# A hybrid HGRN2 and retention layer on one core: places of side transfers, order of the opening, and how the rows of x are scaled

## The chip, the cores and the metric

The kernel runs on one core of one Trainium2 chip. The metric is the device time of one execution in microseconds (us); a kernel's time is the median over runs on the same chip. Engines are named as the profile names them: PE (TensorE, its matrix multiplications), PEld (its weight loads, beside PE), DVE (VectorE), ACT (ScalarE), POOL (GpSimd), SP (SyncE, which here only issues transfers). A "product" below is a group of 12 matmuls of 128x512 on PE, the unit in which the program counts.

## The reference, cut to what matters

SEQ is 2048 and D_MODEL 1024; everything is float32.

```
mod = silu(c) @ w_ada + b_ada ;  shift, scale, gate = split(mod, 3)
h = rms_norm(x, norm_g) * (1 + scale) + shift
proj = h @ w_in            # columns: hq hf hi hz | rq rk rv rz | ga gb
oA = hgrn2_chunkwise(hq, hf, hi, lower_bound)        # 8 heads, state 128x128
qB, kB = rotary(rq), rotary(rk)                      # pairs turned by cos, sin of the position
oB = retention_chunkwise(qB, kB, rv)                 # 8 heads, state 64x128
uA = headRMSNorm(oA) * silu(hz) ; uB = headRMSNorm(oB) * silu(rz)
m = sigmoid(ga) * uA + sigmoid(gb) * uB
x = x + gate * (m @ w_out)
out = rms_norm(x, final_g)
```

Two parts of it are what this case is about. `rms_norm` scales each row (position) of x by its own factor, 1 over the root of the mean square; the projection needs h with the features on the partitions, that is x turned. And `rotary` needs a table of cosines and one of sines over the positions.

## The kernel before, in words

**Tiling.** The positions are worked in two halves of 1024 (`sb` 0 and 1), each of two blocks of 512 (`tb`). Per half, 36 "quads" go one after another; a quad is a group of 256 columns of `w_in`. Its kind is a letter: `a` (hgrn2 q and f), `v` (values), `b` (retention q and k), `A` and `B` (the merge gates and the silu gates). A quad is a 2x2 block product (features in two halves, columns in two), done as seven products by Winograd's scheme: A11, A12, A22 are the blocks of h, S1 to S4 their sums, and `b1` to `b7` are the weights or their sums. Every operand is split into a high and a low part, and each product is three matmuls (high by high, high by low, low by high) for four feature tiles. The products go in the order 2 (of this quad), 7, 1 (of the next), 5, 4, 3, 6. Products 2, 5 and 5+3 leave partial results that later products need: `stash` (L482) copies a PSUM bank to an SBUF tile `c2_`, `c5_` or `c53_` of the ring with the tag `cc` (NCC buffers), and `after` (L495, L502, L506) adds them up. The weights of three products ahead are brought and split (`W.pump`, L421, L295, L296).

**What orders the work.** PE runs in the order in which the program is written: its instructions are pinned. On ACT, DVE, POOL and SP a scheduler chooses the order from dependences and from priorities (the order of the program, shifted by `tc.high_priority(offset=...)`). Buffers are rings by tag: a tile that is asked for while all buffers are in use waits for the last reader of the oldest. `tmp()` gives a tile of the ring `tp` (NTP buffers of 128x512 float32). `cc` and `tp` and `mu` (4 buffers) hold tiles of the same size.

**Lanes and side work.** Between the products, `bg` runs the recurrences as lanes, and one "side" generator at a time, which goes on by one step (one `yield`) per product. The side work of the first half is `next_h(1)` (L1029 on), started in quad 14: it makes h for the second half. For each row tile it loads x (`xt`), squares and sums it on ACT (L1042), makes the diagonal matrix of the factors on POOL (`dgr`, L1047), and multiplies it by ones on PE, so that `rb` holds the factors along the free axis. Then it loads the turned x (`xT`), multiplies by `rb` on DVE (L1058), applies scale and shift on ACT, and stores hT to DRAM. Last it loads hT tiles again and makes S1 to S4 (L1078 on). Between a load and its first use stand two yields. `change_h(1)` loads the sums back in quad 35, the last of the first half.

**Rotation tables.** In a `b` quad, `take_b` (L641) turns a block of q or k: four DVE operations with the tables `ct` and `sn` (L647 to L650). `load_rot` (L630) brings both for one block with transfers issued by POOL (L634, L636): for block 0 at product 2 of the quad, for block 1 at product 2 of the next quad. The turned result of one block is stored by SP (`ro`, or `c` itself; L655).

**The opening.** `opening()` (L1105) works quad 0 without Winograd, and products 1 and 2 of quad 1. Its row tiles of x, `xrow0` to `xrow7`, come by SP. `stats(t)` squares and sums a row tile on ACT (L1116), makes the factor on POOL (`rstd_of`, L174 to L177), and scales the row tile on ACT (L1119). `turned(tb, kt)` turns four 128x128 pieces with PE transposes (L74) into a PSUM bank `xps`, and ACT makes h out of it with scale and shift (L1137). The scale and the shift come from `ada` (L355): DVE multiplies and sums tiles `wa` of `w_ada`, which SP brings, with `scb`, the row of silu(c) that `row_of_c` spreads over the partitions. `prepare` is `ada`, `turned` and the split of h (`split_a`). `plain_step` and `product_step` are the matmuls. After the loop: the two results `after(2, 1)` and `after(1, 1)`, `lower_bounds` (a softmax on ACT and DVE), four `deliver`s (quad 0's results go to ACT at L579 on), and the loading of constants and tables.

## Time and profile before

| | |
|---|---|
| time, median of 3 runs | 2068.94 us (2067.6 to 2070.96) |
| the profiled execution, its own time | 2069.38 us |
| span in it | 2067.6 us |
| granted TensorE clock, mean | 0.982 |
| PE busy | 1948.0 us (94%) |
| PEld busy | 1578.1 us (76%) |
| DVE busy | 1411.8 us (68%) |
| ACT busy | 993.2 us (48%) |
| POOL busy | 271.8 us (13%) |
| bytes moved | 259.95 MB, mean 126 GB/s |

How to read the rows of the trace that follow in the prediction. A row of the timeline has the start in us from the span's start, the duration in us, the engine, the line of the kernel, the operation, `out<-in` by the program's names without numbers, partitions x elements, and the count; brackets at its end hold the time for which the engine stood idle before it and the instruction or transfer that released it. A row of the waits has the waiting operation, what released it, the total in us, how often, and the longest. A row of the windows has a stretch of the span and in it the busy time of each engine (with the instructions), the granted clock as a share of full speed, the share of the DMA engines' time, and GB/s. A row of one line's instructions has the shortest, median and longest duration in ns and the time from the first to the last.

### The profile page before, as it was taken

How to read it: one execution, taken by the hardware profiler on the slowest of the kernel's cores; microseconds unless marked ns; L12 is line 12 of the kernel's file. 1: busy time of each engine (PE TensorE's matmuls, PEld its weight loads, DVE VectorE, ACT ScalarE, POOL GpSimd, SP SyncE). 2: the span in 40 equal slices, each digit the busy share in tenths (PEclk: the TensorE clock that was granted, in tenths of full speed). 3: DMA queues.
4: the chain of work that ended last, by engine and by line, in shares of the span. 5: the costliest groups of instructions: out<-in, count | busy, mean ns of one | idle time of the engine just before them, and what ended most of it. 6: DMA issues, size and time to landing. Idle time of an engine off the chain costs nothing.

```text
span 2067.6 us, 40051 instructions
## 1 busy us (share of the span) xinstructions
PE 1948.0 (94%) x15108; PEld 1578.1 (76%) x15108; DVE 1411.8 (68%) x2677; ACT 993.2 (48%) x2434; POOL 271.8 (13%) x514
## 2 busy tenths in 40 slices
PE   3889899999999889999999999999999999999998
PEld 2668688887787767878777788877788878887887
DVE  4876767676767658586895767677857675768332
ACT  5725454554555434545634545544455445445332
POOL 1001211122013110101001110211011101110000
PEclk9989999999999999999999999999999999999999
DMA  9144524344453565424645424354434433246442
GB/s 305 25 108 120 141 75 108 98 131 131 140 144 114 155 173 168 133 83 138 179 103 130 130 63 109 101 145 136 118 105 124 121 84 117 70 128 188 155 147 86
DMA packets 453120, 259.95 MB, mean 126 GB/s; under 512 B 171712, under 2 KB 406208, under 8 KB 452928
## 3 DMA queue, kind: packets, MB, share of 16 engines
q1 hardware_dynamic: 286752, 172.89, 29.8%
q10 hardware_dynamic: 153120, 76.04, 12.9%
q0 software_dynamic: 13056, 8.47, 1.6%
q8 instruction: 119, 1.95, 0.4%
q14 instruction: 73, 0.60, 0.1%
HBM read 188.03 MB, written 69.21 MB: 124 GB/s over the span
## 4 chain that ended last, share of the span: by engine, by line
PE 39%; DVE 5%; DMA 5%; ACT 2%; issue 1%; POOL 1%; SPq 0%; ACTq 0%; POOLq 0%; DVEq 0%
PE x L71 14%; PE ops L71 8%; PE v L71 7%; PE y L71 3%; PE poh L71 1%; DVE b L296 1%; PE lv L71 1%; DMA ud<-ur 1%; PE rt L71 1%; DMA wg<-in_w_gate_dram 1%; DVE w L421 1%; PE uT L74 1%; PE por L71 1%; ACT b L295 1%; DMA rd<-ro 1%
## 5 line engine op out<-in xcount | busy, mean ns | idle before, releaser
L296 DVE TENSOR_TENSOR b<-w,b 128x512 fp32r<-128x512 f32 (+1 forms) x553 | 346.1, 634 | 291.5 <-ACT b L295 286.2
L71 PE MATMUL v<-S,b 128*128 128x512 f32 x1704 | 429.2, 401 | 11.6 <-ACT c L482 11.3
L71 PE MATMUL x<-S,b 128*128 128x512 f32 x1704 | 433.1, 399 | 2.4 <-DVE c L502 1.3
L71 PE MATMUL x<-A,b 128*128 128x512 f32 x1704 | 425.3, 397 | 6.6 <-ACT c L482 5.8
L295 ACT ACTIVATE b<-w 128x512 fp32r<-128x512 f32 (+1 forms) x553 | 316.6, 583 | 238.1 <-PE x L71 172.8
L71 PEld LDWEIGHTS v<-S,b 128*128 128x128 f32 x1704 | 320.5, 191 | 82.3 <-ACT c L482 15.1
L71 PEld LDWEIGHTS x<-A,b 128*128 128x128 f32 x1704 | 317.9, 190 | 73.5 <-ACT c L482 6.8
L71 PEld LDWEIGHTS x<-S,b 128*128 128x128 f32 x1704 | 312.1, 189 | 64.6 <-DVE b L296 2.0
L71 PE MATMUL y<-A,b 128*128 128x512 f32 x840 | 211.3, 400 | 13.2 <-DVE vt L596 8.6
L421 DVE TENSOR_TENSOR w<-w,w 128x512 f32<-128x512 f32 x284 | 194.6, 685 | 6.1 <-DMA w<-in_w_d_dram 1.7
L71 PEld LDWEIGHTS y<-A,b 128*128 128x128 f32 x840 | 157.8, 192 | 47.0 <-issue 7.2
L71 PE MATMUL ops<-wo,m 128*128 128x512 f32 x768 | 174.8, 390 | 0.0
L71 PEld LDWEIGHTS ops<-wo,m 128*128 128x128 f32 x768 | 144.0, 188 | 30.4 <-DVE m L301 0.4
L174 POOL TENSOR_SCALAR ssh<-ssh 128x1 f32<-128x1 f32 x128 | 46.9, 366 | 756.5 <-ACT uh L837 753.4
L482 ACT ACTIVATE c<-v 128x512 f32<-128x512 f32 x142 | 84.4, 594 | 116.0 <-PE v L71 94.1
L840 ACT ACTIVATE uh<-poh,rrh 128x128 f32<-128x128 f32 x128 | 47.0, 367 | 120.9 <-POOL rrh L177 120.9
L71 PEld LDWEIGHTS lv<-q,k 128*32 128x32 f32 (+1 forms) x5888 | 69.3, 109 | 46.7 <-issue 34.4
L71 PE MATMUL lv<-q,k 128*32 128x16 f32 (+2 forms) x5888 | 80.5, 187 | 21.6 <-DVE ad L798 10.8
L786 DVE TENSOR_TENSOR q<-q,f 128x512 f32<-128x512 f32 x112 | 76.8, 685 | 13.8 <-PE lv L71 13.6
L177 POOL TENSOR_TENSOR rrh<-ssh,mhalf 128x1 f32<-128x1 f32 x128 | 83.0, 648 | 10.5
L502 DVE TENSOR_TENSOR c<-c,x 128x512 f32<-128x512 f32 x71 | 48.7, 685 | 50.8 <-PE x L71 50.4
L176 POOL TENSOR_TENSOR ssr<-ssr,epsx 128x2 f32<-128x2 f32 x64 | 20.9, 326 | 458.7 <-ACT ur L837 458.6
(191 smaller groups left out, 2443.0 us busy)
## 6 DMA issues: line engine op xcount, KB each, us to landing
w<-in_w_d_dram ACTq DMA_DIRECT2D x128, 256.0 KB
w<-in_w_c_dram ACTq DMA_DIRECT2D x66, 256.0 KB
mu<-ud SPq DMA_DIRECT2D x64, 256.0 KB
w<-in_w_a_dram ACTq DMA_DIRECT2D x60, 256.0 KB
wa<-in_w_ada_dram SPq DMA_DIRECT2D x16, 512.0 KB
w<-in_w_b_dram ACTq DMA_DIRECT2D x32, 256.0 KB
vd<-vt SPq DMA_DIRECT2D x128, 64.0 KB
vdr<-vt SPq DMA_DIRECT2D x128, 64.0 KB
```

The lines of the kernel that those rows point to most:

```text
L71: return tc.keep_in_program_order(nc.tensor.matmul(**kw))
L74: return tc.keep_in_program_order(nc.tensor.transpose(**kw))
L174: G.tensor_scalar(out=ss, in0=ss, scalar1=n * EPS, scalar2=None, op0=ALU.add)
L176: G.tensor_tensor(out=ss, in0=ss, in1=eps, op=ALU.add)
L177: G.tensor_tensor(out=dst, in0=ss, in1=mhalf.broadcast_to([P, w]), op=ALU.pow)
L295: S.activation(out=t[0], in_=src, func=AF.Copy)
L296: return V.tensor_tensor(out=t[1], in0=src, in1=t[0], op=ALU.subtract)
L421: V.tensor_tensor(out=out, in0=x, in1=y, op=ALU.add)
L482: S.activation(out=t, in_=ps, func=AF.Copy)
L502: V.tensor_tensor(out=t, in0=t, in1=xb[q], op=ALU.subtract)
L786: V.tensor_tensor(out=qv, in0=qv, in1=tv[:, :, :, 0:1].broadcast_to([P, NU, nb, m]), op=ALU.mult)
L840: S.activation(out=dsts[i], in_=pos[i], func=AF.Copy, scale=rr[:, i : i + 1])
```

## The change

Four things change; the arithmetic of the reference is untouched.

1. Buffers: the ring `cc` has 4 buffers in place of 5, the ring `tp` 6 in place of 5.
2. The opening. The small loads `ng` and `bad` are issued ahead of the rows of x, and rows 4 to 7 behind the first two `wa` loads and the first four `stats`. `row_of_c` and `prepare` are put under a high priority, the four `deliver`s under `PEV` (600). The scaling of the rows on ACT (eight of 128x1024) goes; instead POOL makes for each row tile the diagonal matrix of its factors (`diag`, eight of 128x128, in two of the `mu` buffers), and PE multiplies the piece of x by this diagonal (64 float32 matmuls of 128x128) where it transposed it with the identity (64). `scp1` sits in another PSUM bank, `h0_3` in `tp` and not in `cc`.
3. `next_h`: three yields in place of two between a load and its use for `xt`, `xT` and two of the hT loads, so that a row tile takes 7 steps in place of 6 and the whole 144 in place of 112. The squares (L1042), the multiplications by `rb` (L1058) and three of the sums (L1078 and later) are pinned to the order of the program on their engines. `rb` moves from the ring `mu` to `tp`.
4. `load_rot` of block 1 is issued at product 6 of the same `b` quad, one product ahead of where it was.

```
-NCC = 5
-NTP = 5
+NCC = 4
+NTP = 6
...
+    pin = tc.keep_in_program_order
...
+    ng = const("ng", [P, KT], a["ng_t"])
+    bad = const("bad", [P, 2 * KT], a["bada_t"])
     for t in range(4):
         load_rows(t)
...
-            ps = bank(f"scp{i}", "v")
+            ps = bank(f"scp{i}", ("v", "lv")[i])
...
+    FIRSTS = 2000
...   next_h
-            rb = upool.tile([P, 512], F32, name=f"rb{b}", tag="mu", bufs=4)
+            rb = tmp(f"rb{b}")
...
-                yield
-                yield
+                for _ in range(3):
+                    yield
                 for i in range(2):
-                    S.activation(out=xt[i], in_=xt[i], func=AF.Square, accum_out=ss[:, i : i + 1])
+                    pin(S.activation(out=xt[i], in_=xt[i], func=AF.Square, accum_out=ss[:, i : i + 1]))
...
-                yield
-                yield
-                V.tensor_tensor(out=x, in0=x, in1=rb, op=ALU.mult)
+                for _ in range(3):
+                    yield
+                pin(V.tensor_tensor(out=x, in0=x, in1=rb, op=ALU.mult))
...
-            V.tensor_tensor(out=h22, in0=h21, in1=h22, op=ALU.subtract)
+            pin(V.tensor_tensor(out=h22, in0=h21, in1=h22, op=ALU.subtract))
             keep("S1", h22)
             h11 = load(0, j)
             yield
             yield
-            V.tensor_tensor(out=h21, in0=h11, in1=h21, op=ALU.subtract)
+            yield
+            pin(V.tensor_tensor(out=h21, in0=h11, in1=h21, op=ALU.subtract))
...   the same for h12 and S4
...   opening
-        was = {0: ada_load(0)}
-        scb = row_of_c()
-        was[4] = ada_load(4)
-        for t in range(4, 8):
-            load_rows(t)
+        diag = [upool.tile([P, 512], F32, name=f"diag{i}", tag="mu", bufs=4) for i in range(2)]
+        with tc.high_priority(offset=FIRSTS):
+            scb = row_of_c()
...   stats
-            S.activation(out=xrows[t], in_=xrows[t], func=AF.Copy, scale=r[:, 0:1])
+            G.tensor_scalar(
+                out=diag[t // 4][:, t % 4 * P : (t % 4 + 1) * P], in0=ident, scalar1=r[:, 0:1], scalar2=None, op0=ALU.mult
+            )
...   turned
-                PE.transpose(
-                    out=ps[:, n * P : (n + 1) * P], in_=xrows[4 * tb + n][:, kt * P : (kt + 1) * P], identity=ident
+                t = 4 * tb + n
+                PE.matmul(
+                    out=ps[:, n * P : (n + 1) * P], lhsT=xrows[t][:, kt * P : (kt + 1) * P],
+                    rhs=diag[t // 4][:, t % 4 * P : (t % 4 + 1) * P], start=True, stop=True,
                 )
...
-                x = upool.tile([P, 512], F32, name="h0_3", tag="cc", bufs=NCC)
+                x = tmp("h0_3")
...   prepare: its three steps under tc.high_priority(offset=FIRSTS)
+        was = {0: ada_load(0), 4: ada_load(4)}
         for t in range(4):
             stats(t)
+        for t in range(4, 8):
+            load_rows(t)
...
-        for ch, tb in ((0, 0), (1, 0), (1, 1), (0, 1)):
-            deliver(0, ch, tb, acc[ch, tb])
+        with tc.high_priority(offset=PEV):
+            for ch, tb in ((0, 0), (1, 0), (1, 1), (0, 1)):
+                deliver(0, ch, tb, acc[ch, tb])
...   the loop over the products
-        if m == 2 and QUADS[q - 1][1] == "b":
-            load_rot(q - 1, 1)
+        if kind == "b" and m == 6:
+            load_rot(q, 1)
```

On ACT the opening's rows of the second block before: `sqj` is a square with its sum, `xrow` the scaling of a row tile, `h0_...` the making of h from a turned piece `xps`, `A12` and `A11` the split.

```order
L1137 ACTIVATE h0_0_302<-xps0_4_365,mods_120 128x512
L1119 ACTIVATE xrow4_89<-xrow4_89,x0r4_348 128x1024
L1116 ACTIVATE sqj_259,x0ss5_352<-xrow5_90 128x1024
L295 ACTIVATE A12_0_0_371<-h0_0_302 128x512
L1119 ACTIVATE xrow5_90<-xrow5_90,x0r5_354 128x1024
L1116 ACTIVATE sqj_259,x0ss6_383<-xrow6_91 128x1024
L1137 ACTIVATE h0_1_407<-xps0_1_402,mods_120 128x512
L1119 ACTIVATE xrow6_91<-xrow6_91,x0r6_385 128x1024
L1116 ACTIVATE sqj_259,x0ss7_389<-xrow7_92 128x1024
L295 ACTIVATE A11_0_1_409<-h0_1_407 128x512
L1119 ACTIVATE xrow7_92<-xrow7_92,x0r7_391 128x1024
L1137 ACTIVATE h0_1_0_417<-xps1_0_412,mods_120 128x512
```

The same place on ACT now, from behind the first square of the second block on:

```order
L1142 ACTIVATE h0_0_304<-xps0_0_299,mods_116 128x512
L1117 ACTIVATE sqj_245,x0ss5_354<-xrow5_280 128x1024
L295 ACTIVATE A11_0_0_306<-h0_0_304 128x512
L1117 ACTIVATE sqj_245,x0ss6_385<-xrow6_282 128x1024
L1142 ACTIVATE h0_0_304<-xps0_4_367,mods_116 128x512
L1117 ACTIVATE sqj_245,x0ss7_391<-xrow7_284 128x1024
L295 ACTIVATE A12_0_0_373<-h0_0_304 128x512
L1142 ACTIVATE h0_1_0_419<-xps1_0_414,mods_116 128x512
L295 ACTIVATE A21_0_0_421<-h0_1_0_419 128x512
L1142 ACTIVATE h0_1_409<-xps0_1_404,mods_116 128x512
L295 ACTIVATE A11_0_1_411<-h0_1_409 128x512
```

The four scalings of row tiles are out from between the squares, and the first h of the second block (`h0_1_0`, from `xps1_0`) stands two rows behind the last square, with `h0_1` behind it and not ahead.

On DVE in the first `b` quad (quad 2) before: `q0_0` and `k0_0` are steps of lane 0, `sw0_0_0` and `c2_2` the turning of block 0, `vt0_0_0_1` the turning of values on which a matmul of the lane waits.

```order
L786 TENSOR_TENSOR q0_0_764<-q0_0_764,f0_0_762 128x64x8
L421 TENSOR_TENSOR w3_0_998<-w3_0_998,w3_1_1088 128x512
L647 TENSOR_TENSOR sw0_0_0_1051<-c2_2_967,sn2_0_898 64x512
L421 TENSOR_TENSOR w3_1_1088<-w3_1_1088,w3_3_1090 128x512
L648 TENSOR_TENSOR sw0_0_0_1051<-c2_2_967,sn2_0_898 64x512
L787 TENSOR_TENSOR k0_0_763<-k0_0_763,f0_0_762 128x64x8
L649 TENSOR_TENSOR c2_2_967<-c2_2_967,ct2_0_897 128x512
L790 TENSOR_TENSOR k0_0_763<-k0_0_763,f0_0_762 128x64
L650 TENSOR_TENSOR c2_2_967<-c2_2_967,sw0_0_0_1051 128x512
L791 TENSOR_TENSOR f0_0_762<-f0_0_762 128x2x32
L596 STREAM_TRANSPOSE vt0_0_0_1_1144<-x1_345 128x512
```

The same place on DVE now:

```order
L296 TENSOR_TENSOR b2_3_1148<-w3_2_882,b2_3_1148 128x512
L787 TENSOR_TENSOR q0_0_766<-q0_0_766,f0_0_764 128x128x4
L648 TENSOR_TENSOR sw0_0_0_1053<-c2_2_969,sn2_0_900 64x512
L788 TENSOR_TENSOR k0_0_765<-k0_0_765,f0_0_764 128x128x4
L799 COPY_PREDICATED ad_110<-msk_72,lv0_0_4_1108 128x32x4
L791 TENSOR_TENSOR k0_0_765<-k0_0_765,f0_0_764 128x64
L792 TENSOR_TENSOR f0_0_764<-f0_0_764 128x2x64
L296 TENSOR_TENSOR b7_2_1170<-w2_1_832,b7_2_1170 128x4x64 x2
L597 STREAM_TRANSPOSE vt0_0_0_1_1146<-x1_347 128x512
L503 TENSOR_TENSOR c53_2_1163<-c53_2_1163,x2_996 128x512
L296 TENSOR_TENSOR b1_3_1242<-w3_0_1000,b1_3_1242 128x512
```

The values' turning `vt0_0_0_1` no longer stands behind the whole turning of block 0 (its three other rows come later now), while the first of those four rows, which needs the table `sn2_0`, now stands ahead of the lane's `k0_0` at L788.

On DVE at the turn from quad 23 to quad 24, a `b` quad, before: `xT3_2` and `xT3_3` are side steps, `c2_24` the stash of product 2, `sw0_3_0` the turning of block 0 of quad 24 with the tables `sn24_0` and `ct24_0`, `b3_24` to `b2_25` split weights.

```order
L596 STREAM_TRANSPOSE vt1_6_0_1_7401<-c5_23_7222 128x512
L1058 TENSOR_TENSOR xT3_2_7374<-xT3_2_7374,rb3_6060 128x512
L495 TENSOR_TENSOR c2_24_7376<-x24_7403,c2_24_7376 128x512
L296 TENSOR_TENSOR b3_24_7434<-w24_3_7232,b3_24_7434 128x4x64 x2
L296 TENSOR_TENSOR b6_24_7463<-w24_0_7126,b6_24_7463 128x4x64 x2
L647 TENSOR_TENSOR sw0_3_0_7428<-c2_24_7376,sn24_0_7347 64x512
L648 TENSOR_TENSOR sw0_3_0_7428<-c2_24_7376,sn24_0_7347 64x512
L649 TENSOR_TENSOR c2_24_7376<-c2_24_7376,ct24_0_7346 128x512
L296 TENSOR_TENSOR b2_25_7497<-w25_2_7313,b2_25_7497 128x512
L650 TENSOR_TENSOR c2_24_7376<-c2_24_7376,sw0_3_0_7428 128x512
L1058 TENSOR_TENSOR xT3_3_7425<-xT3_3_7425,rb3_6060 128x512
```

The same place on DVE now:

```order
L597 STREAM_TRANSPOSE vt1_6_0_1_7370<-c5_23_7187 128x512
L496 TENSOR_TENSOR c2_24_7337<-x24_7372,c2_24_7337 128x512
L296 TENSOR_TENSOR b3_24_7397<-w24_3_7197,b3_24_7397 128x4x64 x2
L296 TENSOR_TENSOR b6_24_7426<-w24_0_7096,b6_24_7426 128x4x64 x2
L648 TENSOR_TENSOR sw0_3_0_7391<-c2_24_7337,sn24_0_7314 64x512
L649 TENSOR_TENSOR sw0_3_0_7391<-c2_24_7337,sn24_0_7314 64x512
L650 TENSOR_TENSOR c2_24_7337<-c2_24_7337,ct24_0_7313 128x512
L651 TENSOR_TENSOR c2_24_7337<-c2_24_7337,sw0_3_0_7391 128x512
L296 TENSOR_TENSOR b2_25_7454<-w25_2_7280,b2_25_7454 128x512
L597 STREAM_TRANSPOSE vt0_6_0_1_7452<-x23_7092 128x512
```

The side steps `xT3_2` and `xT3_3` are gone from here: `xT3_0` to `xT3_7` now stand 63 to 110 rows later on DVE, in this quad and those behind it.

More of the change, by code (lines that the diff above doesn't have):

```diff
@@ L133, in tile_hybrid, with load_rows @@
     xwhere = [("f", 1)] + [("k", 2)] * 2 + [("q", 2)] * 2 + [("A", NA)] * 3
-    for t in range(8):
+    def load_rows(t):
         tag, bufs = xwhere[t]
@@ L138, in tile_hybrid @@
         xrows.append(pool.tile([P, n], F32, name=f"xrow{t}", tag=tag, bufs=bufs)[:, 0:1024])
-    def load_rows(t):
         nc.sync.dma_start(out=xrows[t], in_=a["x"][t * P : (t + 1) * P, :])
+    ng = const("ng", [P, KT], a["ng_t"])
+    bad = const("bad", [P, 2 * KT], a["bada_t"])
     for t in range(4):
         load_rows(t)
-    ng = const("ng", [P, KT], a["ng_t"])
-    bad = const("bad", [P, 2 * KT], a["bada_t"])
     lg = upool.tile([P, 256], F32, name="lg", tag="dT", bufs=1)[:, 0 : 2 * H]
@@ L1090, in next_h @@
             yield
-            V.tensor_tensor(out=h12, in0=h12, in1=h11, op=ALU.add)
+            yield
+            pin(V.tensor_tensor(out=h12, in0=h12, in1=h11, op=ALU.add))
             keep("S4", h12)
@@ L1154, in prepare @@
             kt = KO[s]
-            if tb == 0:
-                ada(kt, was.pop(kt), scb)
-            hs[tb, kt] = turned(tb, kt)
-            ats[tb, kt] = split_a(tb, kt, hs[tb, kt])
+            with tc.high_priority(offset=FIRSTS):
+                if tb == 0:
+                    ada(kt, was.pop(kt), scb)
+                hs[tb, kt] = turned(tb, kt)
+                ats[tb, kt] = split_a(tb, kt, hs[tb, kt])
         def plain_step(ps, b, at, kt):
```

## The prediction

> **What bounds the kernel now.** I read the page first. Its head gives the span and what each engine did in it.
>
> ```profile
> span 2067.6 us, 40051 instructions
> PE 1948.0 (94%) x15108; PEld 1578.1 (76%) x15108; DVE 1411.8 (68%) x2677; ACT 993.2 (48%) x2434; POOL 271.8 (13%) x514
> ```
>
> PE bounds the kernel as a whole: no other engine is busy for more than 68%, and PE stands idle for 2067.6 − 1948.0 = 119.6 us. A change that leaves the products alone can only win from these 119.6 us and from a lowered clock. So the question is where they lie. I listed PE's gaps, and then asked for the windows in which they stood close together.
>
> ```profile
> core 0: us, PE busy (x) PEld busy (x) DVE busy (x) ACT busy (x) POOL busy (x), PEclk, DMA share, GB/s
> 0.00:50.00 50.00, 15.36 (x38) 9.49 (x39) 23.07 (x51) 27.62 (x40) 9.32 (x23) 0.90 0.93 307
> 50.00:100.00 50.00, 40.65 (x178) 31.47 (x177) 43.37 (x82) 34.36 (x57) 1.07 (x2) 0.90 0.07 19
> 100.00:145.00 45.00, 35.12 (x416) 27.65 (x414) 31.61 (x64) 12.81 (x28) 4.50 (x8) 0.85 0.55 118
> 480.00:565.00 85.00, 76.55 (x661) 62.34 (x660) 58.67 (x109) 43.79 (x97) 10.69 (x22) 0.96 0.48 137
> 665.00:780.00 115.00, 97.87 (x656) 78.14 (x654) 74.98 (x140) 48.01 (x111) 13.92 (x24) 0.94 0.60 163
> 780.00:1045.00 265.00, 258.52 (x1981) 210.60 (x1979) 199.49 (x370) 140.13 (x329) 27.09 (x51) 0.99 0.47 138
> ```
>
> Idle PE time is window less busy: 34.6 and 9.4 us in the two windows of the opening, 9.9 at the first `b` quad, 8.5 and 17.1 in the two windows with side work and rotation tables, and 6.5 in the long window behind them, where the kernel runs as it should (2.4%). The two side windows also have a lower clock, 0.96 and 0.94 against 0.99. The change touches each of these places.
>
> **The opening (A).** The rows of the timeline that set its pace:
>
> ```profile
> 36.89 1.28 DVE L355 CUSTOM_DVE_ANT_0 wa<-wa,scb,bad 128x1024 f32<-128x1024 f32 x1 [2.25 <-DMA wa<-in_w_ada_dram]
> ...
> 44.81 1.15 ACT L1119 ACTIVATE xrow<-xrow,x0r 128x1024 f32<-128x1024 f32 x1 [0.47 <-POOL x0r L177]
> 46.02 0.48 PE L74 MATMUL xps<-ident,xrow 128*128 128x128 f32 x1 [2.70 <-ACT xrow L1119]
> ...
> 91.84 4.12 PE L71 MATMUL v<-S,b 128*128 128x512 f32 x12
> ```
>
> The second block's first turned piece is complete only with the last scaling on ACT (44.81 + 1.15). The eight scalings go, 8 × 1.15 = 9.2 us of ACT, four of them from the chain of square, factor, scaling that runs through rows 4 to 7. With the squares (1.04 each) in a row behind each other, and three short POOL steps and the diagonal behind the last, my working by hand puts this turn about 10 us earlier. It is not the only limit: DVE waits for `wa` tiles of `w_ada` (36.89), and these loads do not get faster. The four DVE steps of the next feature tile stand behind that, so the next step starts about 8 to 9 us earlier than in the trace. In the second window DVE is busy for 43.4 of 50 us and mostly keeps what it is handed: about 7 of these us are done earlier. So the first full product of the new kind, at 91.84, comes some 7 us earlier.
>
> Against this stands the dearer turn on PE. The price of a transpose and of a float32 matmul of the same size:
>
> ```profile
> 50.11 1.04 PE L74 MATMUL xps<-ident,xrow 128*128 128x128 f32 x8
> 50.90 1.63 PE L71 MATMUL c<-A,bp 128*128 128x512 f32 x6
> ...
> 483.32 0.38 PE L71 MATMUL poh<-vh,k 128*128 128x128 f32 x2
> 483.54 0.39 PE L71 MATMUL poh<-vh,af 128*128 128x128 f32 x2
> ```
>
> Eight transposes fill 0.79 us up to the next row, 0.10 each. A float32 matmul of 128x128 leaves two records, and the next starts 0.22 us later. So 64 × 0.12 = 7.7 us more on PE, spread over the opening. PE's 34.6 + 9.4 us of idle time cover it as long as DVE sets the pace; with the cover gone it would be up to 7.7 us on the path. The making of the eight diagonals on POOL has a near row:
>
> ```profile
> L1047 POOL TENSOR_SCALAR dgr<-ident,xr x8: 622/728/1160, 444.2 to 654.8; 128x128 f32<-128x128 f32 x8
> ```
>
> Eight × 0.73 = 5.8 us on an engine that is busy for 9.3 of the first 50 us: hidden, but for the last one, which is in the chain above. The priorities, the bank of `scp1` and the two small loads change only what stands ahead on ACT, DVE and SP in these 50 us; I price them at nothing beyond the start of the steps. **A is −7**, between 0 (the pace is set by the `w_ada` loads alone, and the dearer turns eat the rest) and −12 (the 10 of the earlier turn and 2 of the idle time behind it).
>
> A rule of the Trainium skill speaks against the new turn: the page "TensorE: Matmul & The Clock Gate", section "Terms", calls the transpose mode four times faster for FP32. The rows give a factor of two (0.10 and 0.22); by the page's factor the addition would be an estimated 64 × 0.30 = 19 us instead of 7.7, and A +5 instead of −7.
>
> **The first `b` quad (B).**
>
> ```profile
> 124.19 0.69 DVE L787 TENSOR_TENSOR k<-k,f 128x512 f32<-128x512 f32 x1
> ...
> 131.26 0.68 DVE L647 TENSOR_TENSOR sw<-c,sn 64x512 f32<-64x512 f32 x1
> ...
> 135.53 0.70 DVE L596 STREAM_TRANSPOSE vt<-x 128x512 f32<-128x512 f32 x1
> 136.38 5.46 PE L71 MATMUL y<-A,b 128*128 128x512 f32 x12 [7.09 <-DVE vt L596]
> ```
>
> PE stands for 7.09 us for one turned block of values, which stands on DVE behind the whole turning of block 0. In the new order it stands ahead of three of the four steps. That alone takes away most of the wait. But the first of the four, which needs the table from DRAM, now stands ahead of it and of the lane's L788, and the table itself is written in the opening, about as late as before. If the table comes later than DVE gets there, DVE stands, and all behind it. So **B is −4**, between 0 (the wait is for the table instead) and −9.9 (all idle time of that window).
>
> **The side windows (C).** Here I looked at the waits between 480 and 780, of which the largest on DVE by a transfer is
>
> ```profile
> DVE xT L1058 <- DMA xT<-in_x_t_dram: 17.3, 5, 5.8
> ```
>
> and at rows that show such waits, and what they do to PE:
>
> ```profile
> 485.42 0.68 DVE L647 TENSOR_TENSOR sw<-c,sn 64x512 f32<-64x512 f32 x1 [5.72 <-issue]
> ...
> 491.56 3.78 PE L71 MATMUL v<-S,b 128*128 128x512 f32 x8 [4.65 <-ACT c L482]
> ...
> 711.40 0.69 DVE L1058 TENSOR_TENSOR xT<-xT,rb 128x512 f32<-128x512 f32 x1 [5.09 <-DMA xT<-in_x_t_dram]
> ...
> 748.56 2.88 PE L71 MATMUL v<-S,b 128*128 128x512 f32 x12
> 753.75 0.63 ACT L579 ACTIVATE sg<-c 128x512 f32<-128x512 f32 x1 [4.81 <-DMA rd<-ro]
> ```
>
> DVE and ACT work in order. A side step that waits for its load holds the weight splits and stashes behind it, and PE follows some us later. One more yield gives the load one more product, 2.88 us. Of five waits of 3.5 us in the mean that takes up to 5 × 2.88 = 14.4 of 17.3. Pinning keeps the scheduler from placing a side step ahead of where its load can have landed. The tables of block 1 come one product earlier too (485.42 is such a wait), and a sixth `tp` buffer removes waits for a slot (753.75 is one). What is there to win: the idle 8.5 + 17.1 = 25.6 less the usual 2.4% of 200 us, 4.9, gives 20.7; and the clock back at 0.99 gives 76.6 × 0.03 + 97.9 × 0.05 = 7.2; together 28. I take two thirds, **C is −18**, between −6 (what the tables and the buffer give alone: one wait of 4.65 × 1.28, the clock's share counted in) and −28.
>
> **What is paid for it (D, E, F).** The side work now takes 144 steps and not 112, and the multiplications of block 3 stand 63 to 110 rows later on DVE. So the loads and sums of hT lie in the window from 780 on, which has only 6.5 us of idle time now. **D is +3**, between 0 and +9.3 (two waits as in row 491.56). The sums are pinned too, and three yields stand ahead of most of them, which is why I stay near the lower end.
>
> The ring of stashes has four buffers in place of five. In a `b` quad a stash is given back only by a store:
>
> ```profile
> 142.57 12.17 SPq L655 DMA_DIRECT2D rd<-c  x4
> ```
>
> Three stashes live in each quad. With five buffers the store has about four products, 11.5 us, before its buffer is asked for; with four, in the tightest case, the one product between the stash of product 5 and the next. Four stores took SP 12.17 us to issue, 3.0 each, a little more than 2.88. So at the eight `b` quads a small wait is likely. **E is +3**, between 0 and +10. **F**, the sixth `tp` buffer in the remaining quads, is −1.
>
> The sum: −7 − 4 − 18 + 3 + 3 − 1 = −24. Against the profiled execution's own 2069.4 us that makes 2045. The median of the three runs, 2068.9, is so near that I make no difference.
>
> **The rivals.**
>
> *The waits persist.* SP issues its transfers in order, and its queue holds stores that wait for results. If the loads come late since SP stands at such a store, one more yield only moves the issue and not the arrival, and pinning makes the wait certain. For it: the xT waits of up to 5.8 us are longer than a product, while two yields already gave two products. Against it: the DMA share in the window is 0.60, so a load that is issued goes through. Then C is −6 and the sum −12: 2057.5. As a second form, the side waits go but come back in the later window: C −6, D +9.3, B and A as before: 2063.8.
>
> *Slower: the stash ring.* The stash on ACT (L482) is the operation for which PE waits most in these windows. If at each of the eight `b` quads the stash waits for a store's landing and PE stands as in row 491.56, that is 4.65 × 1.28 (the clock's share) = 6.0 us each, 48 in all, and the sum is −24 − 3 + 48 = +21: 2090. It decides from (24 + 3) / 8 = 3.4 us per `b` quad on. For it: four buffers, three of them in use, and a store that takes longer than a product. Against it: with five buffers PE's and ACT's waits at L482 all end with another engine's work and none with this store, and in the other 32 quads of each half engines, not stores, give the stashes back.
>
> *The turn at the page's factor.* A matmul in place of a transpose costs 0.40 us instead of 0.22, that is 19 us more on PE: 2045 + 11.5 = 2056.5. The rule is that of the Trainium skill named above; the two rows of the trace speak against it.
>
> **How the numbers follow.** The forecast, the terms as above: 0.60. The waits persist, 2057.5: 0.20; they come back later, 2063.8: 0.08. The stash ring, 2090: 0.09. The dearer turn: 0.03. The time is that of the forecast, 2045. The range goes down to 2028: C at −28 and A and B both some 3 better, with half of D. Up it reaches to 2066: the two cases of persisting waits are inside, the stash ring is out, and little of the forecast lies below. A measurement of this kernel can tell about 0.2%, 4.1 us, from no change. Faster by more than that are the forecast, the persisting waits and the dearer turn: 0.60 + 0.20 + 0.03, and of the 0.08 for 2063.8 (5 us below) half, less 0.04 for the upper ends of these cases: 0.83. Within it are those two pieces of 0.04: 0.08. Slower is the stash ring: 0.09.
>
> **What would show it.** A: the first row with twelve `v<-S,b` matmuls at about 85 and not 91.84, and PE's turns about 0.2 us apart. B: no wait of PE over 3 us between 100 and 145. C: the waits of `xT` on its load under 6 us together, and the clock at 0.98 or more where block 1's side work lies. D and E: PE's idle time from 780 to 1045 below 10 us, and no stash with a DMA as its releaser for longer than 1 us. Wrong would be: an opening as long as before, with PE waiting for `xps` or DVE for `wa`; DVE waiting for `xT` as long as before; or rows of L482 and the sums behind it released by `rd<-c`.

## The result, and the profile after

The changed kernel takes 2060.85 us in the median of 4 runs (2059.39 to 2062.62), the kernel before 2069.95 us (2067.6 to 2073.24, 4 runs). The ratio is 0.9954 with a 95% interval of 0.9939 to 0.9968: 9.5 us faster by the ratio, where 24 were forecast; the time lies in the upper part of the stated range. The head of the page of the profiled execution after:

```profile
span 2057.6 us, 40131 instructions
PE 1950.7 (95%) x15172; PEld 1581.2 (77%) x15172; DVE 1413.2 (69%) x2677; ACT 984.9 (48%) x2426; POOL 284.5 (14%) x522
```

PE's idle time went from 119.6 to 106.9 us, while its busy time rose by 2.7, the 64 matmuls in place of transposes among it. The windows that the prediction showed, of the kernel after:

```profile
core 0: us, PE busy (x) PEld busy (x) DVE busy (x) ACT busy (x) POOL busy (x), PEclk, DMA share, GB/s
0.00:50.00 50.00, 24.25 (x105) 18.11 (x106) 26.22 (x57) 22.60 (x37) 14.43 (x31) 1.00 0.90 302
50.00:100.00 50.00, 40.76 (x188) 31.98 (x187) 42.14 (x82) 33.40 (x57) 1.33 (x3) 0.93 0.16 43
100.00:145.00 45.00, 39.04 (x498) 31.01 (x497) 35.86 (x71) 14.13 (x34) 4.24 (x6) 0.92 0.52 114
480.00:565.00 85.00, 74.75 (x685) 59.89 (x685) 61.05 (x112) 42.58 (x96) 9.99 (x20) 1.00 0.41 120
665.00:780.00 115.00, 106.44 (x769) 86.01 (x768) 76.90 (x147) 50.08 (x116) 18.27 (x30) 0.97 0.54 140
780.00:1045.00 265.00, 257.15 (x1978) 209.15 (x1978) 205.35 (x384) 143.12 (x338) 30.89 (x54) 1.00 0.51 157
```

Two windows are much better, the first of the opening and the one from 665 us. The window from 480 on has more idle time on PE than before (10.2 against 8.5), though its clock is back at 1.00.

Windows cut at fixed times mix the work when the kernel shifts. PE runs in the order of the program, so each matmul of one trace has its counterpart in the other (15,028 of 15,044, the turns left out), and the difference of their starts (PE's lead below) shows where time is won and lost. This table is made from the starts in both traces, one execution of each kernel; executions of one kernel differ by some us among themselves, so steps of 1 or 2 us in it mean little:

| start before, us | lead after, us | what lies between |
|---|---|---|
| 90 | 9.4 | the opening's turns |
| 114 | 2.6 | the splits of S, the first lane |
| 141 | 12.3 | the wait for the turned values is gone |
| 159 | 4.2 | the lane's steps of the same `b` quad |
| 459 | 4.1 | |
| 496 | 10.8 | the side window at the third `b` quad |
| 521 | 1.7 | the same, its end |
| 670 | 4.6 | |
| 762 | 16.2 | the side window at the fourth `b` quad |
| 1041 | 14.9 | |
| 1143 | 17.6 | |
| 1400 | 18.0 | |
| 1477 | 10.6 | the third `b` quad of the second half |
| 2029 | 10.0 | |

The change wins at each place that the prediction named, and loses again right behind three of them; it also loses 7 us in the second half, at a place that the prediction did not name. What the losses are, the rows after show. In the opening and the first `b` quad:

```profile
36.41 1.95 PE L71 MATMUL xps<-diag,xrow 128*128 128x128 f32 x16
...
94.11 2.03 PE L71 MATMUL v<-S,b 128*128 128x512 f32 x3 [4.99 <-ACT S L295]
...
135.09 0.73 PE L71 MATMUL lv<-q,k 128*16 128x16 f32 x64 [3.08 <-DVE f L792]
...
152.02 1.00 PE L71 MATMUL lv<-q,k 128*64 128x64 f32 x16 [2.94 <-DVE k L788]
```

The turns that hold the second block's first piece start at 36.41 and the matmul behind them at 38.12; before, the last of those turns started at 46.02. At 94.11 PE waits 5 us for the splits of S on ACT, which stand behind the quad's deliveries. The wait of 7.1 us for the turned values is gone; two waits of 3 us for the lane's steps on DVE stand in its place.

At the third `b` quad three engines wait in a chain:

```profile
495.34 0.60 ACT L483 ACTIVATE c<-v 128x512 f32<-128x512 f32 x1 [4.28 <-DMA rd<-c]
496.48 0.69 DVE L296 TENSOR_TENSOR b<-w,b 128x512 fp32r<-128x512 f32 x1 [3.79 <-ACT b L295]
...
498.74 1.63 PE L71 MATMUL x<-S,b 128*128 128x512 f32 x6 [3.12 <-DVE c L503]
```

A stash on ACT waits 4.28 us for the store of a turned block, the weight split behind it waits on DVE, and PE waits 3.12 us for the sum behind that. Just before, DVE has turned three tiles (L648 to L651), twelve operations between 481.67 and 492.70. In the trace of before the same twelve were spread over 24 us (472.37 to 496.09).

What came ahead of it is seen on POOL, which issues the table loads. The ring `tp` gives the buffers for the tables, and also for the turned values (`vt`, L596) and all side tiles. The changed kernel:

```profile
477.74 1.30 POOL L637 DMA_DIRECT2D sn<-lin  x2 [8.18 <-DMA vd<-vt]
...
480.03 0.37 ACT L841 ACTIVATE uh<-poh,rrh 128x128 f32<-128x128 f32 x1 [4.16 <-POOL rrh L177]
...
480.95 0.69 DVE L296 TENSOR_TENSOR b<-w,b 128x512 fp32r<-128x512 f32 x1 [3.77 <-ACT b L295]
```

POOL stands for 8.18 us with the early sine table until the store of a turned block gives a buffer back. Its next work, the factor `rrh`, comes late by that; ACT waits 4.16 us for it, and DVE waits 3.77 us for ACT and only then turns the three tiles. In `m_rot`, which is the changed kernel with the tables asked for one product later again, the same table is issued 4 us earlier:

```profile
473.75 1.31 POOL L637 DMA_DIRECT2D sn<-lin  x2 [0.54 <-DVE c L650]
```

The first of the three tiles is turned there at 469.94. That it is not turned before 481.67 in the changed kernel fits the order in which the tiles ask for buffers, but no row shows it. The kernel before has a table load that waits for a buffer of the ring at this place, too:

```profile
474.80 0.79 POOL L634 DMA_DIRECT2D ct<-lin  x1 [6.67 <-DVE sw L648]
```

The 7 us of the second half are lost at the same kind of quad, where another side work brings tiles of `w_gate` (L1253) into the ring `tp`. Between 1360 and 1470 us DVE waits for these tiles for 12.0 to 16.1 us in the eight kernels of this text with early tables (13.1 in the changed kernel), and for 3.5 to 11.0 in the others. From 1400 to 1477 the eight lose 3.5 to 7.4 us of PE's lead; of the others `p_buf` loses 3.7 and none more than 2.0 besides.

The waits for the loads of turned x are down as forecast, from 17.3 us:

```profile
DVE xT L1059 <- DMA xT<-in_x_t_dram: 5.6, 1, 5.6
```

### The profile page after: what moved, and what is told of

It is laid out like the page before. It is cut to its first block, busy times and chain, and to the rows that moved or that the text cites. A ratio compares the mean times of both kernels' runs of the same rounds, so it can differ in the third digit from the quotient of the medians.

```text
span 2057.6 us, 40131 instructions
## 1 busy us (share of the span) xinstructions
PE 1950.7 (95%) x15172; PEld 1581.2 (77%) x15172; DVE 1413.2 (69%) x2677; ACT 984.9 (48%) x2426; POOL 284.5 (14%) x522
## 3 DMA queue, kind: packets, MB, share of 16 engines
q10 hardware_dynamic: 153120, 76.04, 13.1%
## 5 line engine op out<-in xcount | busy, mean ns | idle before, releaser
L71 PE MATMUL v<-S,b 128*128 128x512 f32 x1704 | 430.8, 401 | 10.6 <-ACT S L295 5.0
```

The source lines that it names most:

```text
L71: return tc.keep_in_program_order(nc.tensor.matmul(**kw))
```

## The experiments

All ratios are against the kernel before, run on the same chip beside the kernel, with 95% intervals; 0.001 is 2.07 us. Two theories were set against each other. The first: each part gains what the prediction says, but where DVE or ACT is packed the gain is given back a little later (L), and the side work gains by being moved, not by its longer distance (M). The rivals: the parts' gains reach the end (P), and the distance is what helps (Y).

**The parts alone.** `p_open` is the change's opening alone.

> The kernel before with the change's opening alone (its priorities, the diagonals, the order of the loads; buffers, side work and tables as before). Theory L (the gains are there but are given back a little later, where DVE or ACT is packed): PE reaches the end of the opening's turns some 9 us earlier, loses 5 of them where the splits of S stand behind the four deliveries on ACT, and more in the first b quad; 3 to 6 us faster than before in the end, 2064 to 2067. Rival P (what the opening wins reaches the end, and the later parts lose it): 9 us faster, about 2061.

Measured: 2061.93 us, 0.9957 (0.9940 to 0.9973), 8.9 us faster. That is rival P's number, and as much as the whole change. A wait of 4.68 us at the matmuls with S is there too (at 91.61, ended by a stash on ACT), and still most of the lead reaches the end: 9.3 us at 90, 6.4 at 159, 9.1 at the end. Theory L fell for this part. Which of the opening's edits gives the 8.9 us was not separated; of them only the turn and the deliveries were tested, below.

`p_rot` is one line:

```
-        if m == 2 and QUADS[q - 1][1] == "b":
-            load_rot(q - 1, 1)
+        if kind == "b" and m == 6:
+            load_rot(q, 1)
```

> The kernel before with the tables of block 1 brought one product earlier, and nothing else. Theory L: PE's wait of 7.1 us for the turned values in the first b quad moves to other steps of DVE, which is packed there; the two windows with side work change by under 3 us each; in all within 3 us of before, 2066 to 2072. Rival P (the early table alone removes the waits of the rotary steps): 6 to 10 us faster, 2060 to 2064.

Measured: 2103.65 us, 1.0159 (1.0133 to 1.0186), 33 us slower. Neither theory had that. Its trace, 719 to 735 us, at the fourth `b` quad:

```profile
720.09 0.79 POOL L634 DMA_DIRECT2D ct<-lin  x1 [7.92 <-DMA hT<-xT]
720.39 0.69 DVE L1058 TENSOR_TENSOR xT<-xT,rb 128x512 f32<-128x512 f32 x1 [5.12 <-DMA xT<-in_x_t_dram]
...
726.16 0.45 SPq L1055 DMA_DIRECT2D xT<-in_x_t_dram  x1
...
734.18 0.69 DVE L1058 TENSOR_TENSOR xT<-xT,rb 128x512 f32<-128x512 f32 x1 [5.45 <-DMA xT<-in_x_t_dram]
```

POOL's table load waits 7.9 us for the store of a side tile, that is for a buffer of the ring `tp`. The next load of turned x is issued only at 726.16, and DVE, which has reached its multiplication, waits 5.5 us for it with the weight splits and the turning behind. Waits of this length on turned x stand in the trace of before, too (5.09 us at 711.40 and 5.78 at 743.64). What is new is the order behind it: three tiles are turned in one run from 737.81 to 753.46, and only then comes the step L886 of a lane. PE pays for that:

```profile
753.38 0.28 DVE L886 TENSOR_SCALAR st<-st,f 128x128 f32<-128x128 f32 x1
...
753.72 0.80 PE L71 MATMUL poh<-st,q 128*128 128x128 f32 x2 [9.70 <-DVE st L886]
```

Before, that step stood ahead of the last of the three tiles, and PE did not wait for it:

```profile
731.73 0.29 DVE L886 TENSOR_SCALAR st<-st,f 128x128 f32<-128x128 f32 x1
```

This quad is not the whole of it. By the starts of the matmuls `p_rot` loses 11.3 us against the kernel before at the fourth `b` quad (670 to 780 us), 6.2 at the second (159 to 200), 1.8 at the third (459 to 521), and 5.3 and 6.9 at the third and fourth of the second half (1400 to 1477 and 1600 to 1650).

`p_buf` is `NCC = 4`, `NTP = 6` and `h0_3` in the ring `tp`.

> The kernel before with four stash buffers and six temporary ones (and the one opening tile of the stash ring moved to the other ring, as it must be), nothing else. Theory L: the stash waits on ACT for a store of turned values at one or more b quads, as it does for 4.3 us in the changed kernel; 2 to 7 us slower than before, 2071 to 2076. Rival P (the sixth temporary buffer is what removes waits, and the stash ring costs nothing): 3 to 6 us faster, 2063 to 2066.

Measured: 2067.55 us, 0.9986 (0.9968 to 1.0004), 2.9 us faster, not clear of nothing, and between the two forecasts. One stash on ACT waits for a store of turned values in its trace, for 0.6 us: the smaller ring by itself costs nothing that can be measured.

`p_side` adds the change's `next_h`.

> As p_buf, with the change's side work besides (three yields, the pinned steps, rb in the other ring); opening and tables as before. Theory L: the waits for xT between 665 and 780 us go, which gives 10 us against p_buf, so 2061 to 2066. Rival P (side waits only move into the later quads): the same as p_buf within 3 us.

Measured: 2056.59 us, 0.9933 (0.9909 to 0.9956), 13.9 us faster. 11 of them are against `p_buf`, near the 10 of theory L; its time of 2061 to 2066 was reckoned from a slower `p_buf`.

**The change less one part.** `m_deliver` takes the priority from the four deliveries.

```
-        with tc.high_priority(offset=PEV):
-            for ch, tb in ((0, 0), (1, 0), (1, 1), (0, 1)):
-                deliver(0, ch, tb, acc[ch, tb])
+        for ch, tb in ((0, 0), (1, 0), (1, 1), (0, 1)):
+            deliver(0, ch, tb, acc[ch, tb])
```

> The changed kernel with the four deliveries of quad 0 at the priority they had before. Theory L: PE's wait of 5.0 us for the splits of S at 94 us goes, PE is some 5 us further at 110 us, and part of it is given back in the first b quad; 2 to 5 us faster than the changed kernel, 2056 to 2059. Rival D (the stretch up to 220 us is bound by DVE's sum of work, so that order does not matter): within 1.5 us of the changed kernel.

Measured: 2062.17 us, 0.9964 (0.9950 to 0.9979), the same as the changed kernel. In its trace the 5 us at S are gone, and a wait for the turned values is back:

```profile
87.41 4.60 PE L71 MATMUL v<-S,b 128*128 128x512 f32 x12 [0.69 <-ACT c L483]
...
130.91 3.33 PE L71 MATMUL y<-A,b 128*128 128x512 f32 x7 [5.41 <-DVE vt L597]
```

So rival D's number holds, and the waits trade places: what one order of ACT and DVE takes away at one place comes back at another. D's reason, that DVE's sum of work binds this stretch, is not shown: in `m_deliver` DVE is busy for 30.8 of the 45 us from 100 to 145, and in the changed kernel for 35.9.

`m_turn` turns with the identity; it makes the diagonals but leaves out their use, so the rows of the first half are not scaled.

```
-                PE.matmul(
-                    out=ps[:, n * P : (n + 1) * P], lhsT=xrows[t][:, kt * P : (kt + 1) * P],
-                    rhs=diag[t // 4][:, t % 4 * P : (t % 4 + 1) * P], start=True, stop=True,
-                )
+                PE.transpose(
+                    out=ps[:, n * P : (n + 1) * P], in_=xrows[t][:, kt * P : (kt + 1) * P], identity=ident
+                )
```

> The changed kernel with transposes by the identity in place of the 64 matmuls by the diagonals; the diagonals are still made but not used, so this kernel leaves out the scaling of the rows of the first half by the norms. It prices the dearer turn. Theory L: DVE and the loads set the opening's pace, the 7 us less on PE are covered; within 2 us of the changed kernel, 2059 to 2062. Rival T (the turn is on the path): 5 to 8 us faster, 2053 to 2056.

Measured: 2062.66 us, 0.9966 (0.9952 to 0.9979). The dearer turn costs nothing on the path.

`m_rot` puts the tables back to product 2 of the next quad, `m_rot_dl` the deliveries' priority as well.

> The changed kernel with the tables of block 1 brought at product 2 of the next quad, as before. Theory L: within 3 us of the changed kernel, with other places of the waits near the b quads. Rival P: 5 us or more slower, 2066 and above, since the earlier tables carry the gain around the b quads.

> The changed kernel with the tables at their old place (as m_rot) and the four deliveries at their old priority (as m_deliver); the candidate for the best version. If the two add, 2053 to 2056; if the wait of 5 us for the splits of S is what the opening still loses there and nothing behind takes it back, 2048 to 2051.

Measured: 2054.99 us, 0.9923 (0.9893 to 0.9953), and 2058.41 us, 0.9947 (0.9929 to 0.9965). Both intervals overlap that of the changed kernel; neither kernel is slower without the early tables, against rival P. By the ratios `m_rot` is 6.4 us faster than the changed kernel, more than theory L's 3, and `m_rot_dl` 3.5 us faster than `m_deliver`. `m_rot_dl` missed both of its forecasts: the deliveries' old priority adds nothing here either.

`m_side` takes the old `next_h` (with `rb` in the ring `tp`), `m_pin` only the pins away.

> The changed kernel with two yields and no pinned steps in the side work (rb stays in the ring of temporaries). Theory L: the waits for xT between 665 and 780 us come back and cost 8 to 11 us, 2069 to 2072. Rival P (the sixth temporary buffer and the tables carry the gain there): within 3 us of the changed kernel.

> The changed kernel with nothing pinned in the side work, the yields as changed. Theory M: the pins do nothing of their own, within 3 us of the changed kernel, 2058 to 2064. Rival (the scheduler places the multiplications ahead of their loads' landing again): DVE waits for xT come back, 5 us or more slower, 2066 and above.

Measured: `m_side` 2085.30 us, 1.0083 (1.0053 to 1.0112), 27 us slower than the changed kernel and far more than either theory had: without the new side work the early tables cost nearly as much as in `p_rot`. `y_open_buf`, below, is this kernel without the early tables, but for the ring of `rb`; it has 0.9962, so the tables cost 25 us here, with six buffers in the ring `tp`. In the trace 10.2 of them are lost at the fourth `b` quad (670 to 780 us). `m_pin` 2058.57 us, 0.9952 (0.9938 to 0.9967): the pins do nothing.

**Distance or place.** `x_shift` keeps the old distances and moves the second block's loads; `x_dist` keeps the place and lengthens the distance. Both stand on `p_buf`, with `rb` in the ring `tp` as in the change.

```
x_shift:
+            for _ in range(16 * tb):
+                yield
             for kt in range(KT):
                 x = tmp(f"xT{b}_{kt}")
...
x_dist:
-                yield
-                yield
-                V.tensor_tensor(out=x, in0=x, in1=rb, op=ALU.mult)
+                for _ in range(2 + tb):
+                    yield
+                op = V.tensor_tensor(out=x, in0=x, in1=rb, op=ALU.mult)
+                if tb:
+                    pin(op)
```

> The kernel of p_side (four stash and six temporary buffers, opening and tables as before) with the side work's distances as before (two yields, nothing pinned), but sixteen idle steps ahead of the second block's loads of turned x, which puts its first multiplication behind the b quad at 665 to 740 us, where the change puts it too. Theory M (the side work gained since block 3's loads no longer meet the tables and stores of that b quad in one ring and one queue): as fast as p_side, 2054 to 2060. Rival Y (it gained by the longer distance between load and use): as p_buf, 2065 to 2069.

> The kernel of p_side with three yields and the pin only at the second block's multiplications, so that they start in the b quad at 665 us as before, but with the longer distance. Theory M: the waits at that quad stay, 2064 to 2069. Rival Y: as p_side, 2054 to 2060.

Measured: `x_shift` 2058.45 us, 0.9945 (0.9929 to 0.9962); `x_dist` 2062.62 us, 0.9977 (0.9961 to 0.9993). The moved loads give 8.5 us against `p_buf`, most of `p_side`'s 11, as theory M had it; the longer distance gives 1.9, within the noise, and `x_dist` ends between the two forecasts, nearer to M's. The traces say it more sharply. DVE's waits for turned x between 480 and 780 us, and the window 665 to 780, first of `x_shift`, then of `x_dist`:

```profile
DVE xT L1061 <- DMA xT<-in_x_t_dram: 15.9, 6, 7.8
...
665.00:780.00 115.00, 105.25 (x764) 85.26 (x763) 78.79 (x149) 49.80 (x113) 14.25 (x24) 0.96 0.53 139
```

```profile
DVE xT L1059 <- DMA xT<-in_x_t_dram: 4.8, 3, 2.3
...
665.00:780.00 115.00, 99.43 (x672) 80.74 (x671) 75.58 (x144) 46.08 (x106) 14.91 (x24) 0.93 0.55 150
```

The kernel with three times the waits is the faster one, and PE stands idle for 9.8 us of this window and not 15.6. Where the side steps lie decides. In `x_shift` the last tile of the `b` quad is turned at 717.86 and the second block's first multiplication comes at 726.24; 12.3 of the 15.9 us of waits lie behind the turning. In `x_dist` the second block's steps lie from 675 to 755 among the turnings, and now the turnings wait, for the store of a side tile, that is for a buffer of the ring `tp`:

```profile
702.67 0.69 DVE L648 TENSOR_TENSOR sw<-c,sn 64x512 f32<-64x512 f32 x1 [3.86 <-DMA hT<-xT]
...
730.08 0.69 DVE L650 TENSOR_TENSOR ro<-x,ct 128x512 f32<-128x512 f32 x1 [4.45 <-DMA hT<-xT]
```

These are 8.3 us, against 4.9 in `p_buf` and none in `x_shift`. The longer distance moved the wait from the side step to the turning.

**What adds and what the tables cost.** Four kernels were put together from the parts: the opening with the buffers; the opening with only the sixteen idle steps; with both; and `p_side` with the early tables.

> The change's opening and its buffer counts, side work and tables as before. Theory A (opening and buffers win different times and add): 0.9957 less 0.0014, about 12 us faster than before. Theory R (both take the same wait at the first b quad, where the six buffers alone already brought PE 4.4 us): as the opening alone, 9 us or less.

> The change's opening, buffers of before (five and five), tables as before, and in the side work only the sixteen idle steps ahead of the second block's loads of turned x. Theory A: opening 9 us and shift 8.5 us (x_shift less p_buf) add, 17 to 18 us faster than before. Theory R (what the opening wins is given back before the second half): 9 to 12 us faster.

> As y_open_shift with four stash and six temporary buffers: the change without its earlier tables, its pins and its longer distances. Theory A: 9 and 11.4 us add, 20 us faster than before. Theory R: as m_rot and m_rot_dl, 11 to 16 us.

> The kernel of p_side with the tables of block 1 one product earlier: the change without its opening. Theory T (the earlier tables cost time even with six buffers and the side work out of their way): 4 to 8 us slower than p_side, that is 6 to 10 us faster than before. Rival N (with six buffers they cost nothing): as p_side, 13 to 14 us faster than before.

| kernel | median, us | ratio | 95% interval |
|---|---|---|---|
| `y_open_buf` | 2062.44 | 0.9962 | 0.9948 to 0.9977 |
| `y_open_shift` | 2054.46 | 0.9939 | 0.9917 to 0.9960 |
| `y_open_buf_shift` | 2052.86 | 0.9927 | 0.9906 to 0.9948 |
| `y_side_rot` | 2066.86 | 0.9985 | 0.9972 to 0.9997 |

The buffers add nothing to the opening (theory R). The shift adds to it 7.2 us with the buffers and 3.7 without. `y_open_buf_shift`, 15.1 us faster than before, is in theory R's range, and `y_open_shift`, 12.6, just above it and far below A's 17 (both by the ratios). And `y_side_rot` is 10.8 us slower than `p_side`: theory T's sign, and more than its 4 to 8. In its trace the chain of the changed kernel stands again, at the same quad:

```profile
500.74 0.60 ACT L483 ACTIVATE c<-v 128x512 f32<-128x512 f32 x1 [4.24 <-DMA rd<-c]
...
504.14 3.00 PE L71 MATMUL x<-S,b 128*128 128x512 f32 x12 [3.04 <-DVE c L503]
```

In `p_side` the longest wait of a stash for a store of turned values is 0.6 us. All five kernels with early tables and the new side work (the changed one, `m_deliver`, `m_turn`, `m_pin`, `y_side_rot`) have one of 3.7 to 4.7 us; no kernel without the early tables has one of more than 2.1.

Last, `z_rot_shift` is `p_rot` with the sixteen idle steps, and `z_late` is `y_open_buf_shift` with the tables one product later than before (`if m == 7 and kind == "b": load_rot(q, 1)`).

> The kernel before with two edits: the tables of block 1 one product earlier, as in p_rot, and sixteen idle steps ahead of the second block's loads of turned x, which take them out of the b quad at 665 us. Theory M (the 33 us that the earlier tables cost alone come mostly from their meeting with those loads in the ring of five temporaries): 0 to 10 us slower than before, 2069 to 2079. Rival G (they cost as much at each b quad, whatever runs beside): 20 us or more slower, 2089 and above.

> The kernel of y_open_buf_shift with the tables of block 1 one product later than before the change (the other direction). Theory B (what an earlier table costs is that both blocks are turned in one run on DVE, and the stores and stashes bunch): as fast as y_open_buf_shift or up to 3 us faster, 2050 to 2056. Rival W (the tables' landing is what DVE waits for, so that later is worse): 5 us or more slower than it, 2058 and above.

Measured: `z_rot_shift` 2077.55 us, 1.0052 (1.0031 to 1.0072), 22 us less than `p_rot` and inside M's range of times, but only in part by M's mechanism. At the fourth `b` quad (670 to 780 us) `p_rot` loses 11.3 us against the kernel before and `z_rot_shift` wins 9.5; `x_shift`, without early tables, wins 12.3 there. So the meeting with the side loads costs some 11 us, a third of the 33, and the other half of the 22 is what the move wins anyway. At the other four `b` quads named above `z_rot_shift` loses 20.6 us, as much as `p_rot` (20.2): the larger part of the tables' price lies there. With six buffers in the ring `tp` the six other kernels with early tables lose nothing at the fourth `b` quad of the second half, and 1.0 us at most at the second of the first half. `z_late` 2052.73 us, 0.9921 (0.9903 to 0.9940), as `y_open_buf_shift`: a later table is not waited for to any cost. `z_late` has the lowest ratio of all kernels here, but the best five (`z_late`, `m_rot`, `y_open_buf_shift`, `p_side`, `y_open_shift`) are not told apart by their intervals.

## Why the prediction was wrong, point by point

The sum fails at the term C; the others stay inside their bounds. C was −18 and D +3. Against `y_open_buf`, which has the opening and the buffers, the changed kernel is 1.7 us faster, with C and D together and not clear of the noise: of the 18 us some 2 or 3 came. The time lies between the two forms of the rival of the persisting waits (2057.5 and 2063.8), but by neither mechanism, since the waits for turned x went from 17.3 to 5.6 us and only 1.4 us of PE's lead were lost from 780 to 1041. The ledger from the kernels with the opening, by ratios: opening alone −8.9 us; with the buffers +1.0; with the second block's loads moved −7.2; with the rest of the change (the early tables, the longer distances, the pins) +5.6; together the measured −9.5.

- **A, the opening, −7:** right in size, 8.9 alone. The second block's first turn is complete 8 us earlier where 10 were worked out, the lead of PE at the end of the turns is 9.4 where 7 were, and the dearer turn is covered (`m_turn`). The sixteen records of eight turns take from 36.41 to 38.12, 0.21 us a turn, twice the price of a transpose. By that the rival with the rule of the Trainium skill's page "TensorE: Matmul & The Clock Gate", section "Terms" (a factor of four) falls: the trace does not agree with it.
- **B, the first `b` quad, −4:** the wait of 7.1 us went, but two of 3 us came, and the lead grew there by 1.6 us only (2.6 to 4.2). `m_deliver` shows that the waits there trade places when the order changes. The term was too large, inside its bounds.
- **C, the side windows, −18:** this step failed, in two of its assumptions. First, it took PE's idle time in the two windows for the effect of DVE's waits for turned x, so that a longer distance would win it back. The sign that it named, waits of under 6 us together, came true (5.6), and the gain did not. Against `p_buf`, `x_dist` takes half of them away (9.1 to 4.8 us) and wins nothing that can be measured; `x_shift` raises them to 15.9 and wins 8.5. What wins is the move of the second block out of the `b` quad, which the prediction saw only as a cost (D). Second, it counted the earlier tables as part of the gain. They are a loss: 33 us alone, 25 with the opening and the buffers, 10.8 beside the new side work, and some 6 in the finished kernel (`m_rot` 0.9923, changed kernel 0.9954), where the intervals overlap. The row on which that rested, 485.42, names no releaser but "issue"; the row behind it (487.10) waits 1.00 us for the sine table. That the table load itself stood 6.67 us for a buffer of the ring (474.80), so that an earlier request need not land earlier, was not asked.
- **D, the later window, +3:** PE's idle time there is 7.9 us, below the 10 named, and the lead goes from 16.3 to 14.9 us. Right, in the lower half of its bounds.
- **E, the stash ring, +3:** one chain of 3.1 us at one `b` quad, the rival's mechanism at a small fraction of its price. By itself the ring costs nothing (`p_buf`); the long wait needed the early tables. Two readings under this term were wrong: the row of 12.17 us at 142.57 spans four issues of 0.5 to 1.3 us each with other transfers' time between them, and is no issue time of 3.0 each; and one stash of before waits for a transfer and not for an engine, 3.2 us for the load of `vh`.
- **F, the sixth buffer, −1:** nothing apart from `p_buf`'s 2.9, which isn't clear of zero.

Left open is why the parts do not add fully: opening (8.9) and `p_side` (13.9) would make 23, and the kernels that hold both without the early tables have 11 to 16. Part of it may be the first `b` quad, where opening and buffers each shorten the same wait: in `p_buf` alone PE's lead there rises from 2.4 to 7.9 us, of which 3.2 are left at 159. With intervals of 3 to 6 us on each number the rest wasn't settled.

## What to carry to other kernels

A wait's total in a profile is not its price: ask which work is queued behind the waiting instruction and whether PE is near enough to need it, and consider moving the work to another place before lengthening its distance. A transfer that is asked for earlier takes its buffer earlier, or waits longer for one and holds up the engine that issues it: count who holds the ring between issue and use, and who comes late for it. And where several engines work for one another in a chain, a wait that is removed can come back at the next instruction that needs the same engines.

## What the runs showed of the hardware

The granted clock was low where PE's waits stood close together, but it did not follow their sum alone. In the window from 665 to 780 us it was 0.88 with 24.3 us of idle PE in `p_rot` (the row below), 0.94 with 17.1 before and 0.97 with 8.6 after; but it was 0.96 with 16.7 in `y_open_buf` and 0.93 with 15.6 in `x_dist`, and in the window from 480 on it rose from 0.96 to 1.00 while the idle time rose from 8.5 to 10.2 us. What sets it in these windows was not worked out.

```profile
665.00:780.00 115.00, 90.69 (x564) 72.32 (x563) 68.58 (x126) 43.47 (x107) 12.79 (x23) 0.88 0.51 141
```
